# Attention by pairs of query tiles: eight transposes at a time, one value product over 512 queries, half of the normalisation on GpSimd

## The chip, the cores and the metric

The kernel runs on one core of one Trainium2 chip. The metric is the device time of one execution in microseconds, and what counts is the median of several runs. A core has five engines that work side by side, each through its own instructions in order: PE (TensorE, matrix products and transposes), DVE (VectorE) and ACT (ScalarE), which both read and write PE's accumulators in PSUM, POOL (GpSimd), which here works on SBUF alone, and SP (SyncE), which issues most DMAs. An instruction waits where another engine's result or a free buffer is not there yet, and everything behind it on its engine waits too.

## The reference

One transformer block over 512 tokens of width 1024: a gated linear attention (GLA) branch and an eight-head attention branch with latent projections (MLA), merged, projected, followed by an MLP with a squared ReLU. The change concerns the softmax attention of the MLA branch:

```python
def attend(qblk):
    s = jnp.einsum('bhqd,bhkd->bhqk', qblk, kt).astype(jnp.float32)
    p = jax.nn.softmax(s, axis=-1)
    return jnp.einsum('bhqk,bhkv->bhqv', p.astype(vt.dtype), vt)
```

with 8 heads, 512 queries and 512 keys of 96 features, and values of 128 features. Its output is then gated, added to the GLA branch (`merged`) and multiplied by `w_out`.

## The kernel before

All arithmetic is in float32. A product of two float32 matrices is made of three products in a second 32-bit type: each operand is split into a rounded part (`hi`) and a remainder (`lo`), and `mm3` (L90 to L93) issues hi x hi, hi x lo and lo x hi into one accumulator. `split` (L95) makes the two parts: ACT copies the rounded part, then DVE (or POOL, where the caller says so) subtracts it from the source. So the lines L91, L92, L93 (PE), L96 (ACT) and L97 (DVE or POOL) stand for many different operations, told apart by the names of their tiles.

PSUM has eight banks of 128 x 512 floats. Two tags share them, four banks each: `at` (scores, transposes and small sums) and `mm` (projections, value products `av`, the first half of the out-projection). SBUF tiles come from tags with a fixed number of buffers: `u2` (128 x 512 floats, 25 buffers) and `u4` (128 x 1024, 26 buffers). The order of an engine's instructions is found by a scheduler, which takes the traced program, its dependencies and its buffers and may put an instruction ahead of one that was traced earlier. In some places the program binds the order by hand (`in_program_order`, `goes_behind`); attention is not one of them.

Attention (L733 to L845) runs over 32 steps, four query tiles of 128 for each of eight heads, and six more to run out. A step has up to three parts, each working on a tile of an earlier step:

- `att_scores(head, qt)`: three matmuls of 512 columns make the scores `s` of one query tile in an `at` bank. DVE finds the negated row maximum (`top`, L741), ACT the exponentials `e` with their row sums `tot` (L744), DVE the reciprocal (L745). Then `e` is multiplied by it, on DVE for odd tiles (L747), on ACT for even ones (L749).
- `att_flip(head, qt)`, three steps later (`LAG_B`): four transposes of 128 x 128 (L758) put the probabilities of the tile into one `at` bank `tp`, and `split` takes them out into `pT`, which holds 256 queries.
- `att_values(head, half)`, from six steps later (`LAG_C`), each second step: twelve matmuls of 256 columns multiply the values `v` of the head with the `pT` of a half of its queries, into one half of the `mm` bank `av`. After the second half, DVE gates the result (L775, tile `tb`) and POOL adds the GLA branch (L776).

Between these parts `next(units)` takes a piece of `up_units`, the projections of the next pair of heads: queries `uq` (9 matmuls of 512 columns), keys `uk` (6) and values `uv` (twice 12 of 256), with their splits into `q`, `kbuf` and `v`, the loads of weights, and four copies of rotary rows from `ro` into `q` on SP. The first steps also finish the last GLA head: its sums `gla3ss`, their power on POOL (L268), the factors `gla3dg` on DVE (L276), their spreading `gla3rs` on PE (L285) and two multiplications `g` (L583).

After the loop `merged` is split into `mg` (L846 to L849), and the out-projection `rows_product` (L860) reads it. Its weights `wo00` to `wo13` are loaded and split (`weights`, L221) as soon as their buffers are free, the first of them during attention; some of its matmuls can run there too.

Of the kernel before, what the change touches and what calls it, by code (L numbers as in the profile page):

```python
# [26 lines left out]
MH, NOPE, ROPE, MV = 8, 64, 32, 128  # L27
# [32 lines left out]
def tile_block(ctx: ExitStack, tc: tile.TileContext, t, out: bass.AP):  # L60
    nc = tc.nc
# [5 lines left out]
    def tl(shape, dt, tag, bufs, name):  # L67
        serial[0] += 1
        return sb.tile(shape, dt, tag=tag, bufs=bufs, name=f"{name}_{serial[0]}")

    def u2(name, dt=F32, shape=(P, S)):
        return tl(list(shape), dt, "u2", 25, name)

    def u4(name, dt=F32R, shape=(P, 2, S)):
        return tl(list(shape), dt, "u4", 26, name)

    def sm(name, n=4, dt=F32):
        return tl([P, n], dt, "sm", 24, name)

    def ps(tag, name):  # L80
        serial[0] += 1
        return pp.tile([P, S], F32, tag=tag, bufs=4, name=f"{name}_{serial[0]}")

    def one(shape, dt, name):
        return sb.tile(shape, dt, tag=name, bufs=1, name=name)

    def raw(x):
        return x.bitcast(F32)

    def mm3(acc, lh, ll, rh, rl, start, stop, onto=False):  # L90
        nc.tensor.matmul(acc, lh, rh, start=start, stop=False, skip_group_check=onto)  # L91
        nc.tensor.matmul(acc, lh, rl, start=False, stop=False, skip_group_check=onto)  # L92
        nc.tensor.matmul(acc, ll, rh, start=False, stop=stop, skip_group_check=onto)  # L93

    def split(hi, lo, src, rest=nc.vector):  # L95
        nc.scalar.activation(hi, src, AF.Copy)  # L96
        rest.tensor_tensor(lo, src, raw(hi), op=ALU.subtract)  # L97
# [38 lines left out]
    ident = one([P, P], F32, "ident")  # L136
# [420 lines left out]
    def gla_out(h, sc, v, g1, name):  # L557
        accs = [ps("at", f"{name}o{j}") for j in range(2)]
        for dv in range(2):
            for j in range(NT):  # L560
                at = (h % 2) * GDV + dv * P
                c = slice(at, at + P)
                mm3(accs[dv], v[j][:, 0, c], v[j][:, 1, c], sc[j][:, 0, :], sc[j][:, 1, :],
                    j == 0, j == NT - 1)
        sq = []
        for dv in range(2):
            s = u2(f"{name}sq{dv}")
            nc.scalar.activation(s, accs[dv], AF.Square)
            sq.append(s)
            f = 2 * h + dv  # L570
            nc.vector.scalar_tensor_tensor(
                g1[dv], accs[dv], gla_gain[:, f : f + 1], g1[dv], op0=ALU.mult, op1=ALU.mult
            )
        nc.vector.tensor_tensor(sq[0], sq[0], sq[1], op=ALU.add)
        return sq[0]

    def gla_rstd(sq, g1, name):
        return feature_rstd(sq, GDV, name), g1, name

    def gla_norm(diag, g1, name):  # L580
        rs = spread(diag, name)
        for dv in range(2):
            nc.vector.tensor_tensor(g1[dv], g1[dv], rs, op=ALU.mult)  # L583
        return g1
# [95 lines left out]
    merged = [None] * MH  # L680
# [51 lines left out]

    probs, pTs, avs = {}, {}, {}  # L733

    def att_scores(head, qt):
        q, kb, _, _ = heads[head]
        tok = slice(qt * P, (qt + 1) * P)
        acc = ps("at", f"s{head}{qt}")
        mm3(acc, q[:, 0, tok], q[:, 1, tok], kb[:, 0, :], kb[:, 1, :], True, True)
        top = sm("top", 1)  # L740
        nc.vector.tensor_reduce(top, acc, axis=AX.X, op=ALU.max, negate=True)  # L741
        e = u2(f"e{head}{qt}")
        tot = sm("tot", 1)
        nc.scalar.activation(e, acc, AF.Exp, bias=top, accum_out=tot)  # L744
        nc.vector.reciprocal(tot, tot)  # L745
        if qt % 2:
            nc.vector.tensor_scalar(e, e, tot, None, op0=ALU.mult)  # L747
        else:
            nc.scalar.activation(e, e, AF.Copy, scale=tot)  # L749
        probs[head, qt] = e  # L750

    def att_flip(head, qt):
        e = probs.pop((head, qt))
        if qt % 2 == 0:
            pTs[head, qt // 2] = [u4(f"pT{head}{qt}{x}", F32R, (P, NT, 256)) for x in range(2)]
        tp = ps("at", f"tp{head}{qt}")
        for k in range(NT):
            nc.tensor.transpose(tp[:, k * P : (k + 1) * P], e[:, k * P : (k + 1) * P], ident)  # L758
        hi, lo = pTs[head, qt // 2]
        c = slice((qt % 2) * P, (qt % 2 + 1) * P)  # L760
        split(hi[:, :, c], lo[:, :, c], tp.rearrange("p (k q) -> p k q", k=NT))

    def att_values(head, half):
        if half == 0:
            avs[head] = ps("mm", f"av{head}")
        acc = avs[head]
        hi, lo = pTs.pop((head, half))
        _, _, vs, c = heads[head]
        for k in range(NT):
            vt = vs[k // 2]  # L770
            mm3(acc[:, half * 256 : (half + 1) * 256], vt[:, 0, k % 2, c], vt[:, 1, k % 2, c],
                hi[:, k, :], lo[:, k, :], k == 0, k == NT - 1)
        if half == 1:
            y = g2[head]
            nc.vector.scalar_tensor_tensor(y, y, 1.0, acc, op0=ALU.add, op1=ALU.mult)  # L775
            nc.gpsimd.tensor_tensor(y, y, y1[head], op=ALU.add)  # L776
            merged[head] = y

    y1, g2 = [], []
    z_chunk()  # L780
# [4 lines left out]
    for h in range(GH):  # L785
# [44 lines left out]
    for n in range(4 * MH + LAG_C):  # L830
        if n == 1:
            waiting = gla_rstd(*waiting)
        if n == 4:
            y1 += gla_norm(*waiting)
        if n % 8 == 1 and n // 8 + 1 < MH // 2:
            units = up_units(n // 8 + 1)
        if n < 4 * MH:
            att_scores(n // 4, n % 4)
        next(units, None)
        b = n - LAG_B  # L840
        if 0 <= b < 4 * MH:
            att_flip(b // 4, b % 4)
        c = n - LAG_C
        if c >= 0 and c % 2 == 1:
            att_values(c // 4, (c % 4) // 2)  # L845
# [348 lines left out]
```

## Time and profile before

| what | us |
|---|---|
| median of 3 runs (lowest, highest) | 784.45 (784.42, 784.87) |
| the profiled execution, its own time | 783.52 |
| its span, first to last instruction | 781.8 |
| PE busy in the span | 772.8 |
| first score matmul to the end of the last value matmul | 317.8 to 400.1 |

A profile is one execution, recorded instruction by instruction. A row of its groups gives the line, engine and operation, the tiles written and read, shapes and count, the busy time and the mean length of one, and the idle time of the engine just before, with what ended it. `PEld` is the loading of weights into PE, which runs beside the matmuls. Matmuls are pipelined: a matmul's recorded length runs on while the next has begun, so what one costs is read from the distance of two starts. Idle time of an engine costs nothing unless PE, or the end, waits for it.

### The profile page before, as it was taken

The page shows a single profiled execution, that of the slowest core. Times are in us where ns is not written, and L with a number is a line of the kernel's source. Part 1 is how long each engine was busy: PE and PEld are TensorE (multiplying, and loading weights), DVE is VectorE, ACT ScalarE, POOL GpSimd, SP SyncE. Part 2 cuts the span into 40 slices and gives each one's busy share as a digit, 9 for nine tenths or more (in the row PEclk, how much of TensorE's full clock was granted, in tenths as well). Part 3 has the DMA queues.
Part 4 walks back from the last instruction along what each step waited for, and adds up shares of the span by engine and source line. Part 5 has one row for each costly group of instructions (what it writes and reads, how often), then busy time and mean ns, then how long its engine had stood idle before and what let it go on. Part 6 is the DMA issues. An engine that isn't in the chain of part 4 may idle for free.

```text
span 781.8 us, 10005 instructions
## 1 busy us (share of the span) xinstructions
PE 772.8 (99%) x3736; PEld 648.5 (83%) x3736; DVE 544.2 (70%) x839; ACT 410.1 (52%) x685; POOL 104.1 (13%) x168
## 2 busy tenths in 40 slices
PE   9999999999999999999999999999999999999996
PEld 7888888888888888888888898888888888888885
DVE  7767656576566449799973578874787578848695
ACT  7564624532562236798853366435553455436644
POOL 1023203213021314211120100000000000000014
PEclk9999999999999999999999999999999999999998
DMA  7634133133223411523033731155106411460002
GB/s 247 168 90 111 33 84 106 54 94 107 62 75 82 75 40 51 139 55 108 28 128 88 267 110 54 53 179 145 43 14 208 141 46 35 162 183 6 28 1 108
DMA packets 102385, 74.47 MB, mean 95 GB/s; under 512 B 14976, under 2 KB 86656, under 8 KB 102336
## 3 DMA queue, kind: packets, MB, share of 16 engines
q1 hardware_dynamic: 101248, 70.66, 31.4%
q10 hardware_dynamic: 864, 2.38, 0.8%
q0 software_dynamic: 224, 0.79, 0.3%
q8 instruction: 29, 0.48, 0.3%
q14 instruction: 20, 0.16, 0.1%
HBM read 69.62 MB, written 2.10 MB: 92 GB/s over the span
## 4 chain that ended last, share of the span: by engine, by line
PE 94%; issue 3%; DVE 2%; ACT 1%; POOL 0%; POOLq 0%
PE f L92 8%; PE f L93 7%; PE f L91 7%; PE gx L91 4%; PE gx L93 4%; PE gx L92 4%; PE gv L320 3%; PE gr L91 2%; PE gr L93 2%; PE wo L93 2%; PE wo L91 2%; PE gr L92 2%; PE gz L93 2%; PE za L92 2%; PE gz L91 2%
## 5 line engine op out<-in xcount | busy, mean ns | idle before, releaser
L962 DVE TENSOR_TENSOR w<-w,w 128x1024 f32<-128x1024 f32 x32 | 38.7, 1220 | 0.4
L1137 POOL DMA_DIRECT2D gfin<-in_g_final x1 | 0.7, 653 | 282.6 <-PE f L93 282.6
L744 ACT ACTIVATE e<-s,top 128x512 f32<-128x512 f32 x32 | 21.9, 685 | 6.0 <-DVE top L741 5.0
L909 DVE TENSOR_TENSOR h<-gx,h 128x512 f32<-128x512 f32 x32 | 21.5, 683 | 1.8 <-PE gx L93 1.7
L97 DVE TENSOR_TENSOR pT<-tp,pT 128x512 fp32r<-128x512 f32 x32 | 21.6, 678 | 0.5 <-ACT pT L96 0.4
L741 DVE TENSOR_REDUCE top<-s 128x1 f32<-128x512 f32 x32 | 21.6, 678 | 0.1
L96 ACT ACTIVATE pT<-tp 128x512 fp32r<-128x512 f32 x32 | 18.9, 593 | 3.1 <-PE tp L758 2.9
L758 PE MATMUL tp<-ident,e 128*128 128x128 f32 x128 | 19.2, 273 | 0.1
L91 PE MATMUL av<-pT,v 128*128 128x256 f32 x64 | 19.3, 301 | 0.0
L776 POOL TENSOR_TENSOR tb<-tb,g 128x512 f32<-128x512 f32 x8 | 11.1, 1383 | 56.9 <-DVE tb L775 43.8
L758 PEld LDWEIGHTS tp<-ident,e 128*128 128x128 f32 x128 | 15.3, 140 | 3.9 <-DVE pT L97 0.5
L535 DVE TENSOR_TENSOR za<-za,R 128x512 f32<-128x512 f32 x8 | 5.5, 691 | 18.7 <-PE za L93 18.7
L1015 ACT ACTIVATE fa<-f 128x512 f32<-128x512 f32 x32 | 18.5, 578 | 0.0
L92 PE MATMUL av<-pT,v 128*128 128x256 f32 x64 | 18.4, 288 | 0.0
L93 PE MATMUL av<-pT,v 128*128 128x256 f32 x64 | 18.1, 283 | 0.0
L96 ACT ACTIVATE gbh<-y 128x512 fp32r<-128x512 f32 x16 | 10.1, 634 | 14.0 <-DVE y L1032 14.0
L451 POOL TENSOR_TENSOR qk<-qkf,e3f 128x256 f32<-128x256 f32 x8 | 7.8, 973 | 63.8 <-DVE qkf L443 63.8
L91 PE MATMUL s<-kbuf,q 128*128 128x512 f32 x32 | 13.7, 429 | 0.3 <-DVE pT L97 0.3
L1024 ACT ACTIVATE px<-fa 128x256 f32<-128x256 f32 x32 | 13.4, 418 | 1.0
L96 ACT ACTIVATE b_20h<-w 128x1024 fp32r<-128x1024 f32 x7 | 7.4, 1059 | 12.1 <-PE gx L93 6.0
L96 ACT ACTIVATE b_10h<-w 128x1024 fp32r<-128x1024 f32 x7 | 7.4, 1059 | 12.1 <-PE gx L93 6.0
L96 ACT ACTIVATE b_00h<-w 128x1024 fp32r<-128x1024 f32 x7 | 7.4, 1058 | 12.1 <-PE gz L93 6.0
(1460 smaller groups left out, 2806.9 us busy)
## 6 DMA issues: line engine op xcount, KB each, us to landing
w<-in_w_ff SPq DMA_DIRECT2D x64, 256.0 KB, 3.4
x<-in_xt SPq DMA_DIRECT2D x8, 256.0 KB, 5.3
vw<-in_w_in SPq DMA_DIRECT2D x8, 256.0 KB, 5.4
q<-ro SPq DMA_DIRECT2D x16, 128.0 KB, 4.6
h<-in_x ACTq DMA_DIRECT2D x4, 512.0 KB, 4.9
out<-ms SPq DMA_DIRECT2D x7, 256.0 KB, 2.2
gr0f<-in_w_in SPq DMA_DIRECT2D x1, 512.0 KB, 5.6
za0f<-in_w_in SPq DMA_DIRECT2D x1, 512.0 KB, 6.5
```

Of the source, the lines that this page charges most:

```text
L91: nc.tensor.matmul(acc, lh, rh, start=start, stop=False, skip_group_check=onto)
L92: nc.tensor.matmul(acc, lh, rl, start=False, stop=False, skip_group_check=onto)
L93: nc.tensor.matmul(acc, ll, rh, start=False, stop=stop, skip_group_check=onto)
L96: nc.scalar.activation(hi, src, AF.Copy)
L97: rest.tensor_tensor(lo, src, raw(hi), op=ALU.subtract)
L320: nc.tensor.matmul(v_accs[i], a[:, i * P : (i + 1) * P], b, start=k == 0 and x == 0, stop=k == KD - 1 and x == 2)
L741: nc.vector.tensor_reduce(top, acc, axis=AX.X, op=ALU.max, negate=True)
L744: nc.scalar.activation(e, acc, AF.Exp, bias=top, accum_out=tot)
L758: nc.tensor.transpose(tp[:, k * P : (k + 1) * P], e[:, k * P : (k + 1) * P], ident)
L909: nc.vector.tensor_tensor(hc, acc, hc, op=ALU.add)
L962: nc.vector.tensor_tensor(wq[dst][g], wq[x][g], wq[y][g], op=op)
L1015: nc.scalar.activation(a, acc, AF.Relu)
```

## The change

Attention now goes over 16 steps, each for a pair of query tiles of one head, and four more to run out.

- `att_scores` makes both tiles' scores, one after the other. Their row sums stand in one tile of two columns, so one reciprocal follows both exponentials. The first tile of the pair is normalised by ACT, the second by POOL; DVE normalises none.
- `att_flip` does the eight transposes of the pair into two `at` banks, one for key blocks 0 and 1, one for 2 and 3, each with 256 queries of two key blocks. `pT` is now a tile for each two key blocks with all 512 queries, filled by the two pairs of a head.
- `att_values(head, kp)` multiplies two key blocks with all 512 queries: six matmuls of 512 columns, twice for a head. Both need the transposes of both pairs.
- A step does its scores, a piece of the projections, the value product of an earlier step, a second piece, and the transposes of the pair two steps back. The value products follow four steps after the scores.
- `u4` gets 28 buffers instead of 26, and the room in SBUF for descriptors of DMAs that POOL issues is set to 8192 bytes.

```diff
     def u4(name, dt=F32R, shape=(P, 2, S)):
-        return tl(list(shape), dt, "u4", 26, name)
+        return tl(list(shape), dt, "u4", 28, name)
...
-    def att_scores(head, qt):
+    def att_scores(head, half):
         q, kb, _, _ = heads[head]
-        tok = slice(qt * P, (qt + 1) * P)
-        acc = ps("at", f"s{head}{qt}")
-        mm3(acc, q[:, 0, tok], q[:, 1, tok], kb[:, 0, :], kb[:, 1, :], True, True)
-        top = sm("top", 1)
-        nc.vector.tensor_reduce(top, acc, axis=AX.X, op=ALU.max, negate=True)
-        e = u2(f"e{head}{qt}")
-        tot = sm("tot", 1)
-        nc.scalar.activation(e, acc, AF.Exp, bias=top, accum_out=tot)
+        tot = sm("tot", 2)
+        es = []
+        for x in range(2):
+            qt = 2 * half + x
+            tok = slice(qt * P, (qt + 1) * P)
+            acc = ps("at", f"s{head}{qt}")
+            mm3(acc, q[:, 0, tok], q[:, 1, tok], kb[:, 0, :], kb[:, 1, :], True, True)
+            top = sm("top", 1)
+            nc.vector.tensor_reduce(top, acc, axis=AX.X, op=ALU.max, negate=True)
+            e = u2(f"e{head}{qt}")
+            nc.scalar.activation(e, acc, AF.Exp, bias=top, accum_out=tot[:, x : x + 1])
+            es.append(e)
         nc.vector.reciprocal(tot, tot)
-        if qt % 2:
-            nc.vector.tensor_scalar(e, e, tot, None, op0=ALU.mult)
-        else:
-            nc.scalar.activation(e, e, AF.Copy, scale=tot)
-        probs[head, qt] = e
+        nc.scalar.activation(es[0], es[0], AF.Copy, scale=tot[:, 0:1])
+        nc.gpsimd.tensor_scalar(es[1], es[1], tot[:, 1:2], None, op0=ALU.mult)
+        probs[head, half] = es
...
+    def att_flip(head, half):
+        es = probs.pop((head, half))
         if half == 0:
+            pTs[head] = [[u4(f"pT{head}{kp}{x}") for x in range(2)] for kp in range(2)]
+        banks = [ps("at", f"tp{head}{half}{kp}") for kp in range(2)]
+        for x in range(2):
+            for k in range(NT):
+                at = (k % 2) * 256 + x * P
+                nc.tensor.transpose(banks[k // 2][:, at : at + P], es[x][:, k * P : (k + 1) * P], ident)
+        c = slice(half * 256, half * 256 + 256)
+        for kp in range(2):
+            hi, lo = pTs[head][kp]
+            split(hi[:, :, c], lo[:, :, c], banks[kp].rearrange("p (k q) -> p k q", k=2))
+
+    def att_values(head, kp):
+        if kp == 0:
             avs[head] = ps("mm", f"av{head}")
         acc = avs[head]
...
+        for x in range(2):
+            mm3(acc, vt[:, 0, x, c], vt[:, 1, x, c], hi[:, x, :], lo[:, x, :], kp + x == 0, kp + x == 2)
...
-    LAG_B, LAG_C = 3, 6
+    LAG_B, LAG_C = 2, 3
...
-    nc = bacc.Bacc("TRN2", target_bir_lowering=False, num_devices=1)
+    nc = bacc.Bacc("TRN2", target_bir_lowering=False, num_devices=1, dynamic_dma_scratch_size=8192)
```

The steps of the loop are now:

```python
    for n in range(2 * MH + LAG_C + 1):
...
        if n < 2 * MH:
            att_scores(n // 2, n % 2)
        next(units, None)
        c = n - LAG_C
        if 0 <= c - 1 < 2 * MH:
            att_values((c - 1) // 2, (c - 1) % 2)
        next(units, None)
        b = n - LAG_B
        if 0 <= b < 2 * MH:
            att_flip(b // 2, b % 2)
```

More of the change, by code (lines that the diff above doesn't have):

```diff
@@ L752, in att_flip @@
[L752 to L761, printed above, removed]
@@ L763, in att_values @@
-    def att_values(head, half):
-        if half == 0:
+        tot = sm("tot", 2)
[10 more added lines that the diff above has]
+            es.append(e)
@@ L765, in att_values @@
+    def att_values(head, kp):
+        if kp == 0:
             avs[head] = ps("mm", f"av{head}")
         acc = avs[head]
-        hi, lo = pTs.pop((head, half))
         _, _, vs, c = heads[head]
[L769 to L777, printed above, removed]
+        vt = vs[kp]
+        hi, lo = pTs[head][kp]
+        for x in range(2):
+            mm3(acc, vt[:, 0, x, c], vt[:, 1, x, c], hi[:, x, :], lo[:, x, :], kp + x == 0, kp + x == 2)
+        if kp == 0:
+            return
+        y = g2[head]
+        nc.vector.scalar_tensor_tensor(y, y, 1.0, acc, op0=ALU.add, op1=ALU.mult)
+        nc.gpsimd.tensor_tensor(y, y, y1[head], op=ALU.add)
+        merged[head] = y
```

16 lines of the change are left out of this document (5 added, 11 removed).

## The prediction

> **What bounds the kernel now.** I read the page's shares first, then the chain that ended last, then the busy times of the attention stretch by itself, then the waits there, and last the order of time on PE.
>
> ```profile
> PE 772.8 (99%) x3736; PEld 648.5 (83%) x3736; DVE 544.2 (70%) x839; ACT 410.1 (52%) x685; POOL 104.1 (13%) x168
> ...
> PE 94%; issue 3%; DVE 2%; ACT 1%; POOL 0%; POOLq 0%
> ```
>
> PE is busy 99% of the span, and 94% of the chain that ended last is PE. So only two things can move the end: fewer PE nanoseconds, or fewer and shorter gaps between matmuls. The change touches attention alone; the columns of the next row, for the stretch from the first score matmul to the last value matmul, are busy us (and instructions) of PE, weight loads, DVE, ACT and POOL, then clock, DMA share, GB/s.
>
> ```profile
> 317.60:399.90 82.30, 81.95 (x548) 72.65 (x547) 76.55 (x153) 68.53 (x146) 14.73 (x14) 1.00 0.25 69
> ```
>
> PE is full here too (81.95 of 82.30), but DVE is at 76.55, 93%: the next limit is close. How much of it PE feels is in the table of waits around the stretch (us in total, times, longest):
>
> ```profile
> PEld s L91 <- DVE pT L97: 0.7, 2, 0.5
> PEld tp L758 <- DVE pT L97: 0.5, 1, 0.5
> PEld s L91 <- ACT e L744: 0.4, 1, 0.4
> PE s L91 <- DVE pT L97: 0.3, 1, 0.3
> PEld tp L758 <- DVE g L583: 0.2, 1, 0.2
> ```
>
> These, the longest, sum to 2.1 us, of which DVE ends 1.7. About that much the change can win by making other engines faster.
>
> **The change, part by part.** First PE's own work, from its order of time (start, us, line; a matmul's length overlaps the next, so the cost is the distance between starts):
>
> ```profile
> 314.37 0.40 PE L91 MATMUL gla3o<-sc,gv 128*128 128x512 f32 x1
> ...
> 317.57 0.39 PE L93 MATMUL gla3o<-sc,gv 128*128 128x512 f32 x1
> ...
> 340.23 0.60 PE L758 MATMUL tp<-ident,e 128*128 128x128 f32 x4
> 340.59 0.36 PE L91 MATMUL av<-pT,v 128*128 128x256 f32 x1
> 340.79 0.28 PE L92 MATMUL av<-pT,v 128*128 128x256 f32 x1
> ...
> 345.16 0.28 PE L92 MATMUL av<-pT,v 128*128 128x256 f32 x1
> ...
> 346.46 0.40 PE L91 MATMUL s<-kbuf,q 128*128 128x512 f32 x1
> ...
> 347.16 0.28 PE L91 MATMUL uv<-wk2h,ckvhl 128*128 128x256 f32 x1
> ```
>
> *Values over all 512 queries.* 192 products of 256 columns become 96 of 512. From 345.16 to 346.46 lie eleven steps, 0.118 us each. A 512-column step is 3.20/14 = 0.229 us (gla3o, 314.37 to 317.57) or 0.70/3 = 0.233 us (scores, 346.46 to 347.16). So 192 x 0.118 = 22.7 us becomes 22.0 or 22.4 us: a gain of 0.7 or 0.3, and I take 0.6. It is small because columns set the price: half the instructions is not half the time. The 96 weight loads that go were hidden under matmuls.
>
> *Eight transposes at a time.* All 128 stay. Does a switch from transposes to matmuls cost something that pairs would halve? Four transposes occupy 340.23 to 340.59, and the first product takes 0.20 instead of 0.12 us: 0.36 + 0.08 = 0.44, or 0.11 each, which is their own pace with no switch left over. I take 0 (bounds 0 and, if the 0.08 were a switch, 16 x 0.08 = 1.3 us of gain).
>
> Then the engines that feed PE; the rows are lines of the attention stretch (busy us, mean ns, idle before), the last one of the whole span:
>
> ```profile
> L744 ACT ACTIVATE e<-s,top 128x512 f32<-128x512 f32 x32 | 21.9, 685 | 6.0 <-DVE top L741 5.0 <-DVE tot L745 0.8
> ...
> L96 ACT ACTIVATE pT<-tp 128x512 fp32r<-128x512 f32 x32 | 18.9, 593 | 3.1 <-PE tp L758 2.9
> ...
> L749 ACT ACTIVATE e<-e,tot 128x512 f32<-128x512 f32 x16 | 11.5, 721 | 1.0 <-DVE tot L745 0.9
> L776 POOL TENSOR_TENSOR tb<-tb,g 128x512 f32<-128x512 f32 x8 | 11.1, 1383 | 56.9 <-DVE tb L775 43.8 <-DVE tot L745 13.1
> L747 DVE TENSOR_SCALAR e<-e,tot 128x512 f32<-128x512 f32 x16 | 9.3, 584 | 0.2
> ...
> L179 POOL TENSOR_SCALAR hp<-hp 128x1 f32<-128x1 f32 x4 | 1.2, 299 | 19.8 <-ACT ms L175 19.8
> ```
>
> *Normalisation.* DVE loses the 16 multiplications of L747 (9.3 us) and half of its short reciprocals: 76.55 becomes at most 67.3 of 82 us. ACT keeps its 16 multiplications. The relief can return at most the 1.7 us that DVE ends, and nothing at least. One of those waits (g) comes from work that stays, and the others are on banks that the pairs fill in another rhythm: I take 0.7 of gain.
>
> POOL gets 16 multiplications with one input. None is in the trace; the nearest rows are 0.30 us (one column, L179) and 1.38 us (512 columns, two inputs, L776), and I take 1.3, since the size is L776's. That is 21 us on top of 14.7 of 82, so POOL does not fill up. On POOL a multiplication can stand behind a `tb` addition that waits for a value product; but the flip now comes two pairs (some 10 us) after the scores instead of three tiles (7.7). Where the distance is shortest, at the last pair, PE has about 4 us of products and transposes between that pair's reciprocal and the transposes that need the product of POOL, and POOL spends 1.0 of an addition and 1.3 there: 1.7 us to spare. Cost 0; at the dearer end of 1.4 us still 0. The shared reciprocal makes the first tile of a pair wait for the second tile's exponential, about 0.7 us, inside the same lag.
>
> ```profile
> 384.01 1.29 POOL L776 TENSOR_TENSOR tb<-tb,g 128x512 f32<-128x512 f32 x1 [7.07 <-DVE tot L745]
> ...
> 384.51 1.07 DVE L747 TENSOR_SCALAR e<-e,tot 128x512 f32<-128x512 f32 x1
> ```
>
> POOL can hurt DVE in another way: at 384.51 an L747 that has a mean of 0.584 took 1.07 us, until POOL's addition ended. Other DVE work could be held so too, each time by at most one multiplication; that falls on the 9.3 us just freed (cost 0) and, where it doesn't, is rival 3. The Trainium skill (page "SBUF — State Buffer", section on who interferes with whom) says that DVE instructions with two SBUF inputs, not only the one-input multiplications, share a read port with GpSimd under an exclusive lock; by it the remainders of the out-projection's weights, which have two, would queue behind POOL's multiplications. The rows agree for L747; none here shows it for two inputs.
>
> *Start of attention.* Scores now come two tiles at a time and a pair's two transpose banks are filled together, out of the same four banks.
>
> ```profile
> 323.96 1.28 DVE L741 TENSOR_REDUCE top<-s 128x1 f32<-128x512 f32 x2
> ...
> 329.25 0.68 DVE L97 TENSOR_TENSOR pT<-tp,pT 128x512 fp32r<-128x512 f32 x1
> ```
>
> Back to back, 512-column DVE work starts every 0.6 us (two reductions in 1.28). Before, the first remainder of a transpose starts at 329.25; between it and the first reduction DVE does eight pieces of that size and two multiplications, some 5.6 us. In the built program of the change 14 such pieces stand there, 8.4 us, and a reciprocal that waits for the sixth exponential; so the first remainder starts near 329.25 + 2.8 = 332.0. By its own pieces (eight score tiles, the projections of one pair of heads, eight transposes, from the first score product at 317.8) PE reaches the third bank of transposes near 332.2 and must wait for that remainder to end (0.3 to 0.5 us), then for the next bank, whose remainder stands behind one more reduction and ACT's copy (0.9 us); smaller waits on score banks add 0.4. Against that, before's named waits of this stretch (g, an exponential) go or move. I take +0.9, bounds 0 and 1.6.
>
> *End of attention.* The last two heads have no projections left to put between, so a pair is 1.4 (scores) + 0.9 (transposes) + 1.4 (values) = 3.7 us of PE, and the last value product needs all four query tiles where before it could begin with two.
>
> ```profile
> 397.07 3.75 ACT L100 ACTIVATE mg<-tb 128x512 fp32r<-128x512 f32 x7
> ```
>
> In the new order ACT has four of the `mg` copies (3.75/7 = 0.54 us each, 2.1 together) ahead of the last pair's first copy, and PE has nothing but five out-projection matmuls (5 x 0.229 = 1.1) between that product's first and second matmul. ACT then delivers 0.7 us after PE is ready, and DVE's remainder, behind three `mg` remainders, 0.3 us after the five. One and two pairs earlier the remainder stands behind a reduction of scores that PE has just finished: 0.4 to 0.6 us each. That is 2.0; I take 1.6, since each term rests on queues a few tenths apart. Bounds 0 and 2.5.
>
> *What rides along.* One load of `wo` weights moves ahead of four `q` loads on SP; those are needed some 20 us later. Two more large buffers and a smaller ring for POOL's own DMAs: the one later load of that kind (`gfin`) is needed only in the last quarter of the MLP. After the first out-projection group the order of every engine is that of before. Cost 0.
>
> **Sum.** -0.6 (values) - 0.7 (DVE's relief) + 0.9 (start) + 1.6 (end) = +1.2 us. The profiled execution took 783.52 us, so it would become 784.7; the median of the runs is 784.45, 0.9 above the profiled one, which gives 785.6 us.
>
> **Rivals.** 0.2%, or 1.6 us, is about what a measurement of this kernel can tell from no change: the edges are 782.9 and 786.0.
> 1. *Only the gains.* The start's and the end's queues fit after all, because DVE has over 9 us less to do and PE's waits of before are few. Then 784.45 - 0.6 - 0.7 = 783.2, or with all 1.7 us of DVE's waits gone and 0.7 for the values, 782.1.
> 2. *Four banks are too few for pairs (the other side).* A pair's score banks come free only after two reductions and two exponentials in a row, its transpose banks after two copies and two remainders. Per pair without projections (every fourth, and the last three: six or seven) that is up to 0.5 us more than the 3.7 us of PE cover, so 7 x 0.5 = 3.5 in place of the 1.6 at the end: about 787.5. It decides from the point where ACT's work on such a pair (two exponentials, a multiplication, two copies: 2 x 0.69 + 0.72 + 2 x 0.59 = 3.3, with a few tenths for reading the sums) passes PE's 3.7. Against it: in pairs with projections PE needs 5.3 us (24 x 0.118 and 15 x 0.229 = 6.3 us of projections lie in four pairs).
> 3. *POOL holds DVE up.* Four weight remainders in the stretch, each delayed by one POOL multiplication of 1.3 us: 5.2 us of DVE, of which the freed time covers most; if half reaches PE through late remainders of transposes, +2.6: 788.2.
>
> **How the numbers follow.** Forecast (small loss, own range 784.7 to 786.7) 0.47; rival 1 0.25; rival 2 0.18; rival 3 0.10. Faster by over 0.2% needs the better half of rival 1: 0.13. Same: most of rival 1's rest and two thirds of the forecast, 0.44. Slower: the upper third of the forecast, and rivals 2 and 3, 0.43. The range 782.5 to 788.2 leaves out the best of rival 1 and the worst of rivals 2 and 3.
>
> **What would show it.** Value products 96 times at a 0.227 to 0.235 us pace; DVE at or below 67 us of the attention stretch; POOL rows of about 1.3 us for the multiplication; PE waits on `pT` remainders in the first 18 us and on `pT` copies at the last product. I am wrong if the attention stretch is shorter than 81.5 us (no new waits), if waits are spread over every pair, or if the difference lies outside attention.

## The result, and the profile after

The kernel before took 784.32 us (median of 6 runs, 784.06 to 784.87), the changed one 787.91 us (6 runs, 787.85 to 788.82): a ratio of 1.0047 [1.0035, 1.0060], or 3.6 us slower. The profiled execution took 787.85 us, with a span of 786.1 us against 781.8.

The page of the changed kernel, busy time of each engine and the chain that ended last:

```profile
PE 774.4 (99%) x3640; PEld 643.4 (82%) x3640; DVE 536.7 (68%) x807; ACT 410.2 (52%) x685; POOL 132.0 (17%) x184
...
PE 93%; issue 3%; DVE 2%; ACT 1%; POOL 0%; POOLq 0%; ACTq 0%
```

At this height almost nothing has changed: PE is still 99% busy, DVE has lost 7.5 us and POOL gained 27.9. The attention stretch, from the first score product to the last value products (two of them, of 0.23 us each, lie behind its end here), shows more (busy us and instructions of PE, weight loads, DVE, ACT, POOL; clock, DMA share, GB/s):

```profile
317.60:404.20 86.60, 83.57 (x453) 67.69 (x452) 71.66 (x124) 69.31 (x147) 41.61 (x31) 1.00 0.25 66
```

PE, which was idle for 0.35 us of it, is idle for 3.03. What follows, from there to the end, is the same in the changed kernel

```profile
404.20:786.10 381.90, 375.38 (x1722) 312.03 (x1720) 262.03 (x358) 187.93 (x307) 16.70 (x22) 0.99 0.33 102
```

and in the kernel before:

```profile
399.90:781.80 381.90, 375.35 (x1723) 312.08 (x1721) 264.76 (x361) 188.83 (x309) 17.06 (x22) 0.99 0.33 102
```

As many matmuls are left in both (1722 and 1723), and they take the same 381.90 us, so the 4.3 us lie ahead of that point. Of these, 0.3 us lie ahead of attention as well: the first score product starts at 318.07 us where it started at 317.80, with the same 1469 matmuls ahead of it (in the other profiles below it starts between 317.4 and 318.9, so this is the scatter of single executions). 4.0 us are left for attention. The table of waits in and around it (us in total, times, longest), the rows on which a matmul or its weight load waits:

```profile
PEld av L92 <- DVE pT L97: 4.0, 7, 1.1
...
PEld s L91 <- ACT e L749: 2.1, 6, 0.8
...
PE av L92 <- DVE pT L97: 1.1, 2, 0.7
...
PEld tp L764 <- PE tp L764: 1.0, 1, 1.0
PEld av L91 <- ACT pT L96: 1.0, 2, 0.7
PE tp L764 <- DVE pT L97: 0.8, 1, 0.8
```

The value products (`av`) now wait for the transposed probabilities (`pT`), mostly for DVE's remainder of the split; the waits of before have no such row. The seven waits of the first row stand at the second value product of seven of the eight heads, all but the first. A weight load's wait overlaps the matmul ahead of it, so these rows say who waits for whom, not how much of the end it costs. For the cost I went through the records of PE in the stretch and summed, over all its matmuls, the distance between two starts less the matmul's own pace (0.229 us for 512 columns, 0.118 for 256, 0.110 for a transpose); what is left over is gaps:

```
gaps of PE, us          before   changed   difference
start (to 336.0)         1.1       2.1       +1.0
middle                   1.4       3.0       +1.6
last 10 us               0.1       2.2       +2.1
sum                      2.6       7.2       +4.6
 of it ahead of av       0.0       3.7       +3.7
 of it ahead of tp       0.5       1.2       +0.7
 of it ahead of s        1.5       1.9       +0.4
```

(The rows by product leave out what is under 0.15 us in a part, so they don't add up to the sum.) With 0.7 us less of value products (below) that is +3.9 us, against the 4.0 us found for attention. (The last value product starts 4.6 us later, at 404.4 against 399.8, with two more out-projection matmuls, 0.5 us, done ahead of it, and the 0.3 us from ahead of attention.)

Here is one wait in the middle, from the order of time of the changed kernel (start, length, engine, line):

```profile
377.38 1.03 PE L764 MATMUL tp<-ident,e 128*128 128x128 f32 x8
377.58 0.69 DVE L782 SCALAR_TENSOR_TENSOR tb<-tb,av 128x512 f32<-128x512 f32 x1
...
378.17 0.48 PE L91 MATMUL s<-kbuf,q 128*128 128x512 f32 x1
378.18 1.22 DVE L97 TENSOR_TENSOR wo03l<-wo03f,wo03h 128x1024 fp32r<-128x1024 f32 x1
...
378.29 1.08 ACT L96 ACTIVATE pT<-tp 128x512 fp32r<-128x512 f32 x2
378.35 2.19 POOL L783 TENSOR_TENSOR tb<-tb,g 128x512 f32<-128x512 f32 x1 [4.08 <-DVE tb L782]
...
379.39 1.27 DVE L97 TENSOR_TENSOR pT<-tp,pT 128x512 fp32r<-128x512 f32 x2
...
379.63 0.39 PE L91 MATMUL av<-pT,v 128*128 128x512 f32 x1
380.12 0.50 PE L92 MATMUL av<-pT,v 128*128 128x512 f32 x1
```

The second pair of a head is transposed until 378.2. PE has six score products to do, 1.46 us, and comes to the head's first value product at 379.63, which reads ACT's copy. The second, which reads DVE's remainder, should start 0.229 later, at 379.86, but DVE first finished the previous head (`tb`) and a weight of the out-projection (`wo03l`), so the remainder began at 379.39, and the product starts at 380.12. In the kernel before, half of a head's products needed only its first two tiles, transposed several steps earlier.

And the end of attention, in the same view:

```profile
398.20 1.03 PE L764 MATMUL tp<-ident,e 128*128 128x128 f32 x8
...
399.01 2.38 DVE L101 SCALAR_TENSOR_TENSOR mg<-tb,mg 128x512 fp32r<-128x512 f32 x2
399.06 1.09 ACT L96 ACTIVATE pT<-tp 128x512 fp32r<-128x512 f32 x2
399.18 1.66 POOL L783 TENSOR_TENSOR tb<-tb,g 128x512 f32<-128x512 f32 x1 [2.24 <-DVE tb L782]
399.71 0.50 PE L91 MATMUL av<-pT,v 128*128 128x512 f32 x1 [0.47 <-ACT pT L96]
...
400.97 0.39 PE L92 MATMUL wo<-wo00l,mg 128*128 128x512 f32 x1
401.31 1.28 DVE L97 TENSOR_TENSOR pT<-tp,pT 128x512 fp32r<-128x512 f32 x2
402.05 0.50 PE L92 MATMUL av<-pT,v 128*128 128x512 f32 x1 [0.69 <-DVE pT L97]
```

PE waits 0.47 us for ACT's copy, does one value product and five out-projection products, and waits 0.69 us for DVE, which had two `mg` remainders to do first. These two took 2.38 us; at their usual length (0.68 us, one begun every 0.6) they take 1.28. The second of them began while GpSimd's addition (399.18) ran, and took 1.78 us. By these rows, as an estimate, the remainder of `pT` would have been done some 0.3 us before PE came for it had the addition not stood there; so this last wait has two causes, the place in the order and DVE held up by GpSimd's addition, which is in both kernels.

Three theories for the experiments. **Theory 1**: a value product over all 512 queries needs both pairs' transposes, and stands too close behind the second pair's; the place in the order is the cause. **Theory 2** (rival 2 of the prediction): four score banks are too few for pairs. **Theory 3** (rival 3): GpSimd's multiplication, late by itself and in DVE's way.

### The profile page after: what moved, and what is told of

Read it like the earlier page. It is cut to its first block, busy times and chain, and to the rows that moved or that the text cites. A ratio compares the mean times of both kernels' runs of the same rounds, so it can differ in the third digit from the quotient of the medians.

```text
span 786.1 us, 9826 instructions
## 1 busy us (share of the span) xinstructions
PE 774.4 (99%) x3640; PEld 643.4 (82%) x3640; DVE 536.7 (68%) x807; ACT 410.2 (52%) x685; POOL 132.0 (17%) x184
## 3 DMA queue, kind: packets, MB, share of 16 engines
q10 hardware_dynamic: 864, 2.38, 0.8%
## 4 chain that ended last, share of the span: by engine, by line
PE 93%; issue 3%; DVE 2%; ACT 1%; POOL 0%; POOLq 0%; ACTq 0%
PE f L92 7%; PE f L93 7%; PE f L91 7%; PE gx L91 4%; PE gx L92 4%; PE gx L93 4%; PE gv L320 3%; PE gr L91 2%; PE gr L93 2%; PE za L93 2%; PE gr L92 2%; PE gz L93 2%; PE gz L92 2%; PE gz L91 2%; PE za L91 2%
## 5 line engine op out<-in xcount | busy, mean ns | idle before, releaser
L753 POOL TENSOR_SCALAR e<-e,tot 128x512 f32<-128x512 f32 x16 | 25.4, 1589 | 24.7 <-DVE tot L751 23.2
L747 DVE TENSOR_REDUCE top<-s 128x1 f32<-128x512 f32 x32 | 21.6, 682 | 1.5 <-PE s L93 1.3
L764 PE MATMUL tp<-ident,e 128*128 128x128 f32 x128 | 16.9, 273 | 0.8 <-DVE pT L97 0.8
L92 PE MATMUL av<-pT,v 128*128 128x512 f32 x32 | 13.3, 416 | 1.4 <-DVE pT L97 1.1
```

What stands on the lines that cost most here:

```text
L753: nc.gpsimd.tensor_scalar(es[1], es[1], tot[:, 1:2], None, op0=ALU.mult)
L764: nc.tensor.transpose(banks[k // 2][:, at : at + P], es[x][:, k * P : (k + 1) * P], ident)
```

## The experiments

All kernels of one group ran on one chip with the kernel before beside them, so each ratio is to the runs of before in its own group (medians 783.36, 783.55 and 783.73 us).

**Values one step later.**

```
-    LAG_B, LAG_C = 2, 3
+    LAG_B, LAG_C = 2, 4
```

> The changed kernel, with the value products one step (one pair of query tiles) later; the work is the same. Theory 1 (a value product over 512 queries needs the remainders of both pairs, and stands too close behind the second pair's): the 5.2 us for which the value products' tile waits for the DVE remainder fall below 2, the time falls from 787.9 to 785.0 to 786.2. Theory 2 (score banks: pairs on four banks wait for the exponentials): the waits of scores for the ACT exponential stay or grow, time 787.3 to 788.5. Theory 3 (GpSimd's multiplication, late by itself and holding DVE up): each DVE operation keeps its length, time 787.0 to 788.2.

783.26 us, ratio 0.9998 [0.9989, 1.0007]: the whole loss is gone, with every operation of the change still there. It went below the range of theory 1, which had expected a part of it to stay. What ended the idle time ahead of the value products, of the changed kernel:

```profile
  DVE pT L97: 5.2, 9
  ACT pT L96: 1.4, 3
```

and of this one:

```profile
  ACT pT L96: 0.2, 1
```

By the sum of gaps: ahead of `av` 3.7 us before the shift, 0.0 after it; the last 10 us 2.2 and 0.0; the start 2.1 and 2.1. The scores' gaps stay (1.9 and 1.7, against 1.5 before), and without the value products' wait they cost no time over before: theory 2 falls.

**Half a head's values at a time, in 256 columns, from pairs.** Transposes still in eights, scores in pairs; `pT` is kept by pair.

```
-            pTs[head] = [[u4(f"pT{head}{kp}{x}") for x in range(2)] for kp in range(2)]
+        pTs[head, half] = [u4(f"pT{head}{half}{x}", F32R, (P, NT, 256)) for x in range(2)]
...
-        for x in range(2):
-            mm3(acc, vt[:, 0, x, c], vt[:, 1, x, c], hi[:, x, :], lo[:, x, :], kp + x == 0, kp + x == 2)
+        for k in range(NT):
+            vt = vs[k // 2]
+            mm3(acc[:, half * 256 : (half + 1) * 256], vt[:, 0, k % 2, c], vt[:, 1, k % 2, c],
+                hi[:, k, :], lo[:, k, :], k == 0, k == NT - 1)
```

> The changed kernel, with the transposes still in eights and paired scores, but the values of a half head in twelve products of 256 columns, each of which needs its own pair's transposes alone, which lie two steps back. Theory 1 (lag of the 512-column values): the waits of the value products for the remainder go, but each head pays some 0.6/8 us for the narrower products, 785.0 to 786.3, like the later values. Theory 2 (score banks) and theory 3 (GpSimd): 787.5 to 788.8, since both keep their cause.

783.31 us, 0.9997 [0.9988, 1.0005]. Same place in the order, same banks, same GpSimd; only the need for the second pair is gone, and so is the loss, again all of it, where the expectation had a part. With the experiment above this shows theory 1 from two sides. Its start has 1.0 us of gaps where the changed kernel has 2.1: the first pair's values are there for PE to do while it would wait for a transpose bank.

**Values behind the transposes of a step.**

```
-        c = n - LAG_C
-        if 0 <= c - 1 < 2 * MH:
-            att_values((c - 1) // 2, (c - 1) % 2)
-        next(units, None)
         b = n - LAG_B
         if 0 <= b < 2 * MH:
             att_flip(b // 2, b % 2)
+        next(units, None)
+        c = n - LAG_C
+        if 0 <= c - 1 < 2 * MH:
+            att_values((c - 1) // 2, (c - 1) % 2)
```

> The changed kernel, with the value products of a step behind that step's eight transposes instead of ahead of them: they stand eight transposes (0.9 us) farther behind the transposes they need, half a dose of the later values. Theory 1 (lag of the value products): the 5.2 us of waiting for the remainder fall to between 1 and 3.5, and the time stands 1 to 3 us above the kernel before instead of 3.6. Theory 2 (score banks): 3.2 us or more above it, as nothing is changed for the banks.

783.78 us, 0.9999 [0.9991, 1.0008]: no half recovery but a whole one. The expectation counts the dose too small: beside the eight transposes, the six value products of the step before now also lie between in the source (0.9 + 1.4 us), and a piece of the projections where there is one. On PE, the work between the last transposes and the first value product rises from 1.4 to 3.6 us for the third head and from 1.4 to 2.7 for the fifth; for the last three heads the scheduler chose other orders, with 0.7 to 1.4 us. The wait of the value products for DVE is gone altogether (only ACT's copy is left, 1.2 us of idle in 2 waits). In its place PE stands once for GpSimd: a transpose at 395.23 us waits 1.1 us for the multiplication (L753).

**Values ahead of the scores of a step.**

```
+        c = n - LAG_C
+        if 0 <= c - 1 < 2 * MH:
+            att_values((c - 1) // 2, (c - 1) % 2)
         if n < 2 * MH:
             att_scores(n // 2, n % 2)
         next(units, None)
-        c = n - LAG_C
-        if 0 <= c - 1 < 2 * MH:
-            att_values((c - 1) // 2, (c - 1) % 2)
         next(units, None)
```

> The changed kernel with the value products of a step ahead of that step's scores, so that a head's first value product comes right behind the transposes of its second pair. A dose in the other direction. Theory 1 (lag of the value products): each of the eight heads loses up to the 1.4 us of the six score products that stood between, so 8 to 15 us above the kernel before, with ten or more us of waiting for the pT copies and remainders. Theory 2 (score banks): 3 to 5 us above it, as the changed kernel, since the banks are taken in the same order.

788.81 us, 1.0062 [1.0049, 1.0074], 5.1 us above before: in the direction of theory 1, but far short of its 8 to 15, and just above the 3 to 5 of theory 2. The interval overlaps that of the changed kernel (1.0047 [1.0035, 1.0060]), so this dose by itself decides little. The order of time of this kernel shows why it fell short:

```profile
386.65 0.49 PE L91 MATMUL av<-pT,v 128*128 128x512 f32 x1 [0.47 <-ACT pT L96]
...
387.32 0.50 PE L91 MATMUL s<-kbuf,q 128*128 128x512 f32 x1 [0.18 <-ACT e L749]
387.65 0.39 PE L92 MATMUL s<-kbuf,q 128*128 128x512 f32 x1
...
387.88 0.40 PE L93 MATMUL s<-kbuf,q 128*128 128x512 f32 x1
388.11 0.40 PE L92 MATMUL av<-pT,v 128*128 128x512 f32 x1
```

The order in the source is not the order on PE. For five of the eight heads the scheduler still put three to six score products between a head's last transposes and its first value product, and for seven it put other products (here three of scores) between the first and the second value product, so the remainder was covered and mostly ACT's copy was waited for (4.5 us of idle in 9 waits, against 0.5 in one for DVE); the gaps moved to the scores (2.4 us ahead of `s` in the middle, against 1.1).

**The second tile's normalisation back on DVE**, in the changed kernel and with the values one step later:

```
-        nc.gpsimd.tensor_scalar(es[1], es[1], tot[:, 1:2], None, op0=ALU.mult)
+        nc.vector.tensor_scalar(es[1], es[1], tot[:, 1:2], None, op0=ALU.mult)
```

> The changed kernel, with the second tile's normalisation on DVE as before, not on GpSimd. Theory 1 (lag of the value products too short): no better, as the remainders now queue behind 0.58 us more of DVE work per pair, 787.5 to 788.8. Theory 2 (score banks): 787.5 to 788.3. Theory 3 (GpSimd is late or holds DVE up): the first transposes of a pair's second tile come earlier by about 1.0 us each and the DVE remainders shorten, 785.0 to 786.5.

> The changed kernel with the value products one step later and the second tile's normalisation on DVE. It tells what the GpSimd multiplication is worth once the value products don't wait. Theory 1 (the DVE work mattered only because the value products stood right behind the remainders): 0 to 0.9 us above the kernel before. Rival (moving the multiplication to GpSimd is worth 2 us at any lag): 1.5 to 2.5 us above it.

The first took 789.28 us, 1.0079 [1.0065, 1.0093], the second 784.58 us, 1.0012 [1.0004, 1.0021]. Without GpSimd's part the change is worse, not better, and above the range of every theory: theory 3 falls as the cause of the loss. By the ratios GpSimd's multiplication was worth 0.0032 x 784 = 2.5 us where the value products stood right behind DVE's remainders, and 0.0014 x 784 = 1.1 us where they did not. The intervals, of about 1 us and more on each side, don't tell these two apart, and the second kernel, 1.0 us above its kernel before, lies between the ranges of theory 1 and of the rival. The gaps of PE say that they are alike: 9.2 us against the changed kernel's 7.2, and 4.5 against 2.9 with later values, most of both differences ahead of the scores (1.3 and 1.1 us) and little ahead of the value products (0.2 and 0.1). Waits of the first of the two kernels:

```profile
PEld av L92 <- DVE pT L97: 2.9, 3, 2.3
...
PE av L92 <- DVE pT L97: 2.2, 2, 2.0
```

One value product alone stood 2.0 us for a remainder, ahead of which DVE's multiplication took 1.51 us beside an addition of GpSimd.

**GpSimd's part alone, in the kernel before**, for one tile of two and for three of four:

```
         if qt % 2:
-            nc.vector.tensor_scalar(e, e, tot, None, op0=ALU.mult)
+            nc.gpsimd.tensor_scalar(e, e, tot, None, op0=ALU.mult)
```

```
-        if qt % 2:
-            nc.vector.tensor_scalar(e, e, tot, None, op0=ALU.mult)
+        if qt:
+            nc.gpsimd.tensor_scalar(e, e, tot, None, op0=ALU.mult)
```

> The kernel before, with the normalisation of every second tile on GpSimd instead of DVE, nothing else. GpSimd's multiplication takes 1.57 to 1.6 us and its tile is transposed three tiles later, so theory 1 expects no harm: 0 to 1.0 us below the kernel before. Theory 3 (GpSimd is late or holds DVE up): 0.8 us above it or more, with DVE operations beside GpSimd's longer than in the kernel before.

> The kernel before with three tiles of four normalised by GpSimd (24 instead of none), ACT keeping the first of each head. It takes 4.7 us of GpSimd's time in each head's 10.3 us, and 8 copies of about 0.6 us off ACT beside the 16 multiplications off DVE. If the relief goes on paying: 0.5 to 1.5 us below the kernel before. If GpSimd is late (its weight remainders and additions stand in the same queue): 1 us above it or more, with transposes that wait for the multiplication.

One of two: 782.95 us, 0.9990 [0.9981, 0.9999]. It has the lowest ratio of all versions, 0.6 us below before in the medians; the interval hardly leaves out no change, and overlaps those of the other versions without a loss. Three of four: 785.33 us, 1.0017 [1.0008, 1.0026], and PE waits for GpSimd itself:

```profile
PEld tp L758 <- POOL e L747: 2.6, 4, 1.1
PE tp L758 <- POOL e L747: 1.3, 2, 0.9
```

**Wide values by single tiles.** The kernel before, with the values of a head in twelve products of 512 columns, six of them two steps after its fourth tile is transposed and six two steps later (it also has the 28 buffers and the smaller scratch, which cost nothing by themselves, as the last experiment shows). A tile's transposes then fill two `pT` buffers, so each copy and remainder comes in two pieces of 256 columns.

```
+        for kp in range(2):
+            hi, lo = pTs[head][kp]
+            split(hi[:, :, c], lo[:, :, c], tp[:, kp * 256 : kp * 256 + 256].rearrange("p (k q) -> p k q", k=2))
...
+        if 0 <= c < 4 * MH and c % 2 == 0:
+            att_values(c // 4, (c % 4) // 2)
```

> The kernel before (scores, normalisation and transposes tile by tile, DVE normalises every other tile), with the values of a head for all 512 queries in six products of 512 columns, the first two steps after the head's fourth tile is transposed. Theory 1 (only the lag was at fault, the wide products are no loss): no waits of the value products but at the end, 783.3 to 784.9. Theory 2 (the pairs' score banks) and theory 3 (GpSimd): the same, since neither cause is in it. If wide products lose time by themselves: 785.5 or more.

788.39 us, 1.0062 [1.0049, 1.0074]: a miss. It would count against wide products, were it not for the first experiment, where they are as fast as the narrow ones of the second. The suspect was the pieces, so the kernel before was run with them alone (values of 256 columns, in their old place):

```
-        split(hi[:, :, c], lo[:, :, c], tp.rearrange("p (k q) -> p k q", k=NT))
+        for k in range(2):
+            j = slice(2 * k, 2 * k + 2)
+            split(hi[:, j, c], lo[:, j, c], tp[:, 256 * k : 256 * k + 256].rearrange("p (k q) -> p k q", k=2))
```

> The kernel before, with the ACT copy and the DVE remainder of each tile's transposes in two pieces of 256 columns instead of one of 512 (32 more operations on each engine). It tells why the wide values by single tiles (5.0 us above before) were slow. If it was those pieces: 2.5 to 5 us above the kernel before, with PE waiting at the start of attention. If it was that all values came two tiles later: within 1 us of the kernel before.

787.4 us, 1.0047 [1.0034, 1.0061]: the pieces cost 3.9 us by themselves. The lines of it (busy us, mean ns):

```profile
L97 DVE TENSOR_TENSOR pT<-tp,pT 128x256 fp32r<-128x256 f32 x64 | 25.7, 414 | 1.5 <-ACT pT L96 1.0
...
L96 ACT ACTIVATE pT<-tp 128x256 fp32r<-128x256 f32 x64 | 23.2, 384 | 7.1 <-PE tp L758 5.5 <-DVE pT L97 1.4
```

Half the columns take 0.414 and 0.384 us where 512 took 0.678 and 0.593: 4.1 us more on DVE and 4.3 on ACT, in a stretch where both were 83 to 93% busy. The gaps of PE rise from 2.6 to 6.7 us, 4.4 of them in the middle and not, as was expected, at the start. So the pieces by themselves cost nearly as much as the miss (3.9 and 5.0 us, with overlapping intervals). The two are not the same loss in two sizes, though: the miss has 4.5 us of gaps at the start, where PE has no value products yet (1.3 with the pieces alone), and 2.8 in the middle (4.4). How much of the start comes from the values' later place was not run.

**Transposes in the order of the banks**, with the values one step later:

```
-        for x in range(2):
-            for k in range(NT):
+        for kp in range(2):
+            for x in range(2):
+                for k in (2 * kp, 2 * kp + 1):
```

> The changed kernel with the value products one step later, and the eight transposes in the order of the two banks (both tiles for bank 0, then both for bank 1) instead of in the order of the tiles. The third transpose's 0.8 us wait for a bank at the start of attention moves to the fifth. If that bank wait is a whole loss: 0.2 to 0.6 us below the kernel before. If the second tile, which GpSimd hands over late, is now what the transposes wait for: up to 1 us above it.

783.85 us, 0.9997 [0.9988, 1.0006]. The wait of 0.8 us for a bank stays whole, and so does the time. No gain and no loss.

**The buffers and the smaller scratch alone, in the kernel before:**

```
-        return tl(list(shape), dt, "u4", 26, name)
+        return tl(list(shape), dt, "u4", 28, name)
...
-    nc = bacc.Bacc("TRN2", target_bir_lowering=False, num_devices=1)
+    nc = bacc.Bacc("TRN2", target_bir_lowering=False, num_devices=1, dynamic_dma_scratch_size=8192)
```

> The kernel before with the 28 buffers and the smaller scratch of the change alone, so that the loads that wait for a buffer go out earlier. Within 0.5 us of the kernel before, by every theory; 1 us or more on either side would mean that part of the 3.6 us came from the buffers and not from attention.

783.75 us, 1.0000 [0.9991, 1.0009]. Nothing of the 3.6 us is from there.

## Why the prediction was right, and where it was wrong

The forecast was a small loss inside attention, 785.6 us in a range of 782.5 to 788.2; it is a loss of 3.6 us, inside the range, above the forecast's own range of 784.7 to 786.7. The direction and the place were right, and a late remainder was the right mechanism. That the wider range held is in part luck: its upper end was there for rivals 2 and 3, and the time came near it by neither. One of the forecast's own signs of being wrong was waits spread over every pair, and the waits of the value products came in seven of eight heads. By its steps:

- *Values over 512 columns, -0.6.* Right. In the changed kernel the last value products go on at their pace:

```profile
402.62 0.39 PE L91 MATMUL av<-pT,v 128*128 128x512 f32 x1
...
404.45 0.39 PE L93 MATMUL av<-pT,v 128*128 128x512 f32 x1
```

 Eight steps in 1.83 us are 0.229 each; 96 of them are 22.0 against 22.7 us. It is worked out, not isolated: between the two versions without waits (512 and 256 columns) the runs tell no difference.

- *Transposes in eights, 0.* No more than the gaps at banks was seen of them; not run by themselves.

- *DVE's relief, -0.7.* Right as a size, as far as the intervals go: 0.6 us alone in the kernel before, 1.1 us with late values, 2.5 by the ratio in the changed kernel (about 2 by the gaps). DVE's 71.66 us of the stretch miss the forecast's 67 or less; six `mg` remainders (4.9 us) lie in the longer stretch, where before three did (2.0 us).

- *GpSimd's multiplication, 1.3 us at no cost.* The size was wrong, the cost right:

```profile
L753 POOL TENSOR_SCALAR e<-e,tot 128x512 f32<-128x512 f32 x16 | 25.4, 1589 | 24.7 <-DVE tot L751 23.2 <-PE tp L764 1.5
```

 1.59 us is above even the forecast's dearer end of 1.4, yet no matmul waited for it in the changed kernel. The spare time was there at 16 tiles, and not at 24 (785.33 us).

- *Start, +0.9.* Right in the sum, +1.0, and in one of its terms: the first remainder stood at 332.29 (forecast near 332.0), and the second transpose bank of the next pair waited for a remainder:

```profile
332.29 0.69 DVE L97 TENSOR_TENSOR pT<-tp,pT 128x512 fp32r<-128x512 f32 x1
...
334.48 0.63 PE L764 MATMUL tp<-ident,e 128*128 128x128 f32 x4 [0.79 <-DVE pT L97]
```

 That gap is 0.95 us where 0.9 was forecast. PE came to the bank ahead of it at 333.03, not 332.2, and lost only 0.14 us there instead of 0.3 to 0.5; and the score banks' gaps are 0.8 us in both kernels, neither more nor gone. That these misses cancel is luck.

- *End, +1.6.* Right mechanism, the size +2.1: copy and remainder of the last pair late by 0.47 and 0.69 us (forecast 0.7 and 0.3), around the five out-projection products that it named. The 0.69 is the forecast's queue of `mg` remainders (two, not three), lengthened by GpSimd's addition. Of the two waits of 0.4 to 0.6 us that it expected one and two pairs earlier, one of 0.4 us lies in these 10 us, at 395.57.

- *The pairs between: nothing but the relief, -0.7.* **This is the step that failed.** The forecast looked for a late remainder only at the last pairs, where no projections lie between. Measured: +1.6 us of gaps, and ahead of the value products alone +1.7. Of the 3.1 us between the forecast's +1.2 and the span's +4.3, this step is 2.3, the end 0.5 and the start 0.1; 0.3 lie ahead of attention, and the values gave 0.1 more than was forecast. For the heads between it had put at nothing that a value product waits; but the value products of a step come ahead of its second piece of projections, so that for the third, fifth and sixth heads only six score products (1.4 us) lie between a head's last transposes and its first value product, and DVE had other work ahead of the remainder.

- *What rides along, 0.* Right for the buffers and the scratch (1.0000); the moved load was not run by itself.

- *The rivals.* Rival 2 named 787.5 us, close to what came, by a mechanism that the runs refute: paired scores on four banks, in both experiments that kept them and took the value products' wait away, cost nothing. Rival 3 had the sign of GpSimd's part wrong: without it the kernel is slower. DVE held up by GpSimd does occur (0.46 us of one weight remainder, 1.1 us of one `mg` remainder ahead of the last wait), but the longer one is behind an addition that was there before. Rival 1's "only the gains" is what the kernel with later values should have shown; its 783.26 against 783.36 is less than the 1.2 us of that rival; the start's gaps, which remain (2.1 us against 1.1), are most of that.

- *Two readings of rows of before.* The forecast lets the L747 of 384.51 end with POOL's addition; by the rows it ended 0.28 us after it (385.58 against 385.30). And a row that shows a DVE operation with two SBUF inputs held by GpSimd was there to be read, at 401.34 us (last section).

## What to carry to other kernels

Before making an operation wider, ask what its first instruction now needs, and how much work of the same engine lies between that need and the instruction; a product over all tiles can start no earlier than the last tile, and an order that was good for halves can then be too tight. Here the loss was mended by the order and not by a faster engine: one step later returned all 3.6 us, while the other engines' operations stayed what they were. Read the order from the trace, since the scheduler may not keep that of the source. And the number of pieces on ACT and DVE counted where both were near full: the same columns in twice the instructions cost 3.9 us.

## What was not expected of the hardware

GpSimd's 128x512 multiplication by a number per partition took 1.57 us in its common case (1.562 to 1.922 us in the changed kernel), longer than its two-input addition of the same size (mean 1.38 us before, 1.27 to 1.30 where nothing disturbed it) and 2.7 times the mean of DVE's, 0.584.

DVE was slowed beside GpSimd in operations with two inputs from SBUF too. The kernel before has a case, just behind attention:

```profile
400.73 4.19 DVE L101 SCALAR_TENSOR_TENSOR mg<-tb,mg 128x512 fp32r<-128x512 f32 x5
...
400.90 1.67 POOL L776 TENSOR_TENSOR tb<-tb,g 128x512 f32<-128x512 f32 x1 [2.69 <-DVE tb L775]
```

Five remainders begun every 0.6 us would take 3.1 us. The second, at 401.34, took 1.78 us where the others take 0.68, and ended 0.55 us behind GpSimd's addition. In the changed kernel the same happens at 399.61, and this behind a multiplication:

```profile
344.45 1.57 POOL L753 TENSOR_SCALAR e<-e,tot 128x512 f32<-128x512 f32 x1
344.55 1.67 DVE L97 TENSOR_TENSOR wo00l<-wo00f,wo00h 128x1024 fp32r<-128x1024 f32 x1 [1.02 <-PE tp L764]
```

The other three such remainders take 1.21 to 1.22 us. The Trainium skill (page "SBUF — State Buffer", section "Who interferes with whom") says that such a pair shares a port under an exclusive lock, so that the later one waits for the whole of the other. For GpSimd's addition the trace agrees, with either of the two ahead: the `mg` remainders above lost 1.10 us of an overlap of 1.23, and the addition at 378.35 above came behind the start of `wo03l`'s remainder and took 2.19 us, where undisturbed ones take 1.27 to 1.30; the 0.9 us more are nearly the 1.05 for which that remainder went on. For the multiplication it doesn't: 1.47 us of overlap cost DVE 0.46. In the kernel with three tiles of four on GpSimd, weight remainders that began 0.26 and 0.50 us behind the start of a multiplication lost 0.29 and 0.05 us, and one that began 0.64 us behind it lost nothing. All four fit a multiplication that holds DVE for its first 0.55 us only, which is an estimate from these rows.

Little of this reached PE. In the changed kernel the remainder of `pT` behind `wo00l`'s came late enough for a value product to start 0.11 us late (347.47 us), and the `mg` remainder of 399.61 stands ahead of the 0.69 us wait at the end. The version with later values has two such `mg` remainders (a mean of 0.954 us, 0.834 before) and is no slower than before.

The granted clock fell in one stretch of one profile, that of the kernel with wide values by single tiles, where PE was busy for 13.04 of 15 us:

```profile
330.00:345.00 15.00, 13.04 (x62) 10.29 (x62) 12.94 (x34) 12.05 (x33) 2.26 (x4) 0.89 0.29 70
```

In it, behind an idle time of 1.1 us, score products start 0.43 us apart instead of 0.229 (333.57 to 336.7 us), which makes about 1.3 of that kernel's 4.5 us of gaps at the start (an estimate from these starts). Idle time alone didn't bring it here: the changed kernel with the normalisation on DVE was busy for 12.88 us between 375 and 390, with one wait of 2.0 us, and shows 1.00. What brought it stays open.
